# A step of the attention that takes two pieces of filling work, one unit earlier; query norms behind a weighing; four sums of a down projection behind the next weight chunks

## The chip, the cores and the metric

One core of a Trainium2 chip runs the whole program. The metric is the device time of one execution in microseconds (us); three timed runs of the kernel before gave 1322.02, 1323.74 and 1325.03. The engines are TensorE (PE, with its weight loads shown as PEld), VectorE (DVE), ScalarE (ACT), GpSimd (POOL) and SyncE (SP), which issues most transfers.

## The reference

A trunk of two layers on 512 tokens of width 1024, in float32. Layer 0 is a Mamba-2 mixer and a convolutional feed-forward block (ConvFFN); layer 1 is differential attention and a ConvFFN. Cut to what the change touches:

```python
def diff_attention(x, k, v, rel_bias, ...):
    q = rms_norm((rms_norm(x, ln_g) @ q_w).reshape(b, s, 8, 2, 64), q_norm_g)
    ...
    logits = jnp.einsum('bqhcd,bkhcd->bhcqk', qblk, k) * scale + bias     # causal mask
    p = jax.nn.softmax(logits, axis=-1)
    attn = p[:, :, 0] - lam * p[:, :, 1]          # two maps per head
    o = jnp.einsum('bhqk,bkhd->bqhd', attn, v)
    return (rms_norm(o, subln_g) * (1.0 - lam_init)).reshape(b, s, 1024) @ out_w

def conv_ffn(x, ln_g, up_w, conv_w, conv_b, down_w):
    u = causal_dwconv(rms_norm(x, ln_g) @ up_w, conv_w, conv_b)
    gate, up = u[..., :2816], u[..., 2816:]
    return (jax.nn.silu(gate) * up) @ down_w
```

## The kernel before

**Numbers.** Every matrix product is split: a weight chunk of 128x1024 is loaded (`wr_...`), ScalarE rounds it to a high half `wh_...`, VectorE subtracts to get the low half `wl_...`, and TensorE adds up three products (high by high, high by low, low by high). `chunk` (with `emit_chunk`, `Weights.split` or, for down weights, `combine`) issues the loads and splits of a chunk two chunks ahead of its use; three buffers each hold raw, high and low halves.

**Attention (layer 1).** TensorE's order here is the order of the code (`tc.manual_schedule`); the other engines' orders are made by a scheduler from the code's order and the dependencies. The 8 heads are worked off as 24 units: `Unit(h, part)`, where part 0 holds query blocks 0 and 1, part 1 block 2 and part 2 block 3. A unit passes through `logits` (products `lg`, L1498; VectorE adds the bias and takes maxima, L1504; ScalarE exponentials, L1512), `weigh` (VectorE joins the two maps, L1525, once per query block), `turn` (TensorE transposes into `at`, L1534) and `values` (products `po`, L1545, copied to `ot`, L1548). When the three units of a head are done, `normed_out` normalises the head's output `ot` (VectorE, L1558), and `turned_out` transposes it (`oT`, L1564; copies `oh` and `ol`, L1567 and L1568).

Between these small pieces TensorE does filling work: `fill` is a chain of generators for the projections `v0`, `q1`, `v1` and the first half of the output projection. Each `next(fill)` inside `proj` runs the products of one weight chunk for two of the four token blocks: twelve products (`ps_v_0` and `ps_v_1`, or `ps_v_2` and `ps_v_3`). The names `wh_v_0`, `wh_v_2` and so on count the k blocks of a chunk. A list of numbers in the loop over units (`for places in [...]`) says how many pieces each step takes. A step runs `turn` of the unit before, `logits`, `weigh`, `values` of an older unit, and then its pieces; `out_of` runs `turned_out` for a head that is due, ahead of the piece where the step has one piece, and behind its first piece where it has two.

`head_norm` belongs to `q1`, the queries of heads 4 to 7: it takes the root (`rsqrt_act`, factor `ssq`), multiplies four tiles `knq` by it on VectorE (L1350), and puts the transposes `ktq` (L1357) with their copies `qT` (L1358) into a list `late`; `proj` runs an entry of it when its place, a pair (first k block, token block), is reached. For `q1` the places are (2, 0) and (2, 1), so the transposes stand between the products of the second chunk of `v1`.

**Down projection of layer 1.** `ffn` works in three parts of feature blocks, (0, 6), (6, 14) and (14, 22). At the end of each part `down_tokens` multiplies by the down weights with seven products instead of eight (a Strassen-like scheme): `m` runs over "1257634"; the sums of products go to the residual `xr` and to a running sum `run_sum`, by VectorE (helper `add`, L1139). Products have lines L1133, L1135 and L1136. For `m == "6"` each of the two token blocks gets five sums; the last two of them, into `xr` of block 2 + b, are read by nothing near. All engines' orders here are the scheduler's.

Of the kernel before, what the change touches and what calls it, by code (L numbers as in the profile page):

```python
# [9 lines left out]
F32 = mybir.dt.float32  # L10
# [3 lines left out]
ALU = mybir.AluOpType  # L14
# [4 lines left out]
P = 128  # L19
# [3 lines left out]
NT = T // P  # L23
# [18 lines left out]
def trunk_kernel(ctx: ExitStack, tc, x, ssm_ln_g, ssm_in_w, ssm_conv_w, ssm_conv_b, ssm_dt_bias,  # L42
# [950 lines left out]
    def ffn(l, norm, bp, gnext, nnext):  # L993
        with tc.tile_pool(name="ffn_h%d" % l, bufs=1) as hp, tc.tile_pool(name="ffn%d" % l, bufs=1) as fp:
# [65 lines left out]
            def combine(key, m, p0, c, nq):  # L1060

                n = nq * ncol
                if m == "2" or (m == "4" and not l):
                    t = wrp.tile([P, 1024], F32, tag="raw", name="wr_" + key)
                    sync.dma_start(view(t, nq), source(p0, c, nq, 1, 0 if l or m == "2" else 1))
                elif l:
                    t = raws["x" if m == "7" else "y" if m == "3" else "z"][c // 2]
                    if m == "7":
                        dve.tensor_tensor(out=t[:, :n], in0=t[:, :n], in1=raws["y"][c // 2][:, :n], op=ALU.add)
                else:  # L1070
                    t = raws["x" if m in "17" else "z"][c]
                wh = wp.tile([P, 1024], F32R, tag="wh", name="wh_" + key)
                wl = wp.tile([P, 1024], F32R, tag="wl", name="wl_" + key)
                act.activation(wh[:, :n], t[:, :n], AF.Copy)
                dve.tensor_tensor(out=wl[:, :n], in0=t[:, :n], in1=wh[:, :n].bitcast(F32), op=ALU.subtract)  # L1075
                ready.append((key, view(wh, nq), view(wl, nq)))
                more = ({"1": (0, 1), "5": (1, 1), "6": (1, 0)} if l else {"1": (0, 1), "5": (0, 0), "6": (1, 0)}).get(m)
                if more:
                    plus(t, p0, c, nq, *more)
# [41 lines left out]
            def down_tokens(p0, n, sides, last):  # L1121

                nq = n // 2
                side = {"1": 0, "2": 1, "4": 2, "5": 3, "6": 4, "7": 5, "3": 6}

                def products(m, bs, qs, pss, first=True, end=True, cols=slice(0, 512)):

                    for low in range(2):
                        for b in bs:
                            for q in qs:  # L1130
                                h, w = (t[:, side[m], b * P:(b + 1) * P] for t in sides[q][:2])
                                if low:
                                    pe.matmul(pss[b], h, ws[q][1][:, cols], start=False, stop=end and q == qs[-1])  # L1133
                                    continue
                                pe.matmul(pss[b], h, ws[q][0][:, cols], start=first and q == qs[0], stop=False)  # L1135
                                pe.matmul(pss[b], w, ws[q][0][:, cols], start=False, stop=False)  # L1136

                def add(t, v, op=ALU.add):
                    dve.tensor_tensor(out=t, in0=t, in1=v, op=op)  # L1139

                def to(b, c, n=512):
                    return xr[:, b, c:c + n]

                def store(b, c, eng):
                    eng.dma_start(out[0, b * P:(b + 1) * P, c:c + 256], to(b, c, 256))

                def stores(bs, c):
                    for b in bs:
                        for j in range(2):
                            store(b, c + 256 * j, sync if j else act)  # L1150

                for m in SEVEN[1]:
                    pss = [(aux_bank if m in "273" else mm_bank)("ps_s%s_%d_%d" % (m, p0, b)) for b in range(2)]
                    cut = last and m == "4"
                    ws = {}
                    for q0 in range(0, nq, 2):
                        wh, wl = chunk("s1%s_%d_%d" % (m, p0, q0))
                        qs = range(q0, min(nq, q0 + 2))
                        for q in qs:
                            ws[q] = wh[:, q - q0, :], wl[:, q - q0, :]  # L1160
                        if not cut:
                            products(m, range(2), qs, pss, q0 == 0, qs[-1] == nq - 1)
                    if cut:
                        products(m, (0,), range(nq), pss)
                    for b in range(2):
                        r = run_sum[:, b, :]
                        if m == "1":
                            add(to(b, 0), pss[b])
                            act.activation(r, pss[b], AF.Copy)
                        elif m == "2":  # L1170
                            add(to(b, 0), pss[b])
                        elif m == "5":
                            add(to(b, 512), pss[b])
                            add(to(2 + b, 512), pss[b])
                        elif m == "7":
                            seven = pss
                        elif m == "6":
                            add(r, pss[b])
                            add(to(b, 512), r, ALU.subtract)
                            add(r, seven[b])  # L1180
                            add(to(2 + b, 512), r, ALU.subtract)
                            add(to(2 + b, 0), r)
                        elif m == "3":
                            add(to(b, 512), pss[b])
                        elif not (cut and b):
                            add(to(2 + b, 0), pss[b])
                    if last and m in "263":
                        stores((2, 3) if m == "6" else (0, 1), 0 if m == "2" else 512)
                    if cut:
                        stores((2,), 0)  # L1190
                        products(m, (1,), range(nq - 1), pss)
                        add(to(3, 0), pss[1])
                        for j in range(2):
                            end = aux_bank("end%d" % j)[:, :256]
                            products(m, (1,), [nq - 1], {1: end}, cols=slice(256 * j, 256 * (j + 1)))
                            add(to(3, 256 * j, 256), end)
                            store(3, 256 * j, act if j else sync)
# [85 lines left out]
    with tc.tile_pool(name="att", bufs=1) as ap, ExitStack() as later:  # L1283
# [61 lines left out]

        def head_norm(key, kn, ss, dst, gcol, where):
            rsqrt_act(ss, ap, key, [P, NT, 8], 64)
            for b in range(NT):
                v = kn[b].rearrange("p (a q) -> p a q", a=8)
                dve.tensor_tensor(out=v, in0=v, in1=ss[:, b, :].unsqueeze(2).to_broadcast([P, 8, 64]),  # L1350
                                  op=ALU.mult)

            def turned(bs):
                for b in bs:
# [263 lines left out]
        with tc.manual_schedule(engines={mybir.EngineType.PE}):  # L1618
# [51 lines left out]
                    values(valued)  # L1670
                    valued += 1

            for places in [(2, 2), 1, 1, 1, 1, 1, 1, 1, 1, 1, 2, 1, 1, 1, 1, 2, 1, 2, 1, 2, 1, 2, 2, 1, 1, 1]:
                if isinstance(places, tuple):
                    weigh_to(t)
                    turn_to(t - 1)
# [76 lines left out]
```

## Time and profile before

| what | value |
|---|---|
| timed runs | 1322.02, 1323.74 (median), 1325.03 us |
| the profiled execution's own time | 1323.59 us |
| its span, first to last instruction | 1321.9 us |
| mean granted TensorE clock | 0.999 |
| DMA mean | 127 GB/s |

The span is shown beside the own time because rows of the trace count from the span's start. TensorE's busy share is 99%, but a busy TensorE is not one at its peak: products are pipelined, and the trace's ends of products are modelled. So progress is read from the starts of products, and losses from the list of waits and from places where starts come further apart. In a timeline's row stand the start, the duration, the engine, line and operation, the tiles written and read, shapes and count, and in brackets the idle time ahead of it with what ended it.

### The profile page before, as it was taken

How to read it: one execution, taken by the hardware profiler on the slowest of the kernel's cores; microseconds unless marked ns; L12 is line 12 of the kernel's file. 1: busy time of each engine (PE TensorE's matmuls, PEld its weight loads, DVE VectorE, ACT ScalarE, POOL GpSimd, SP SyncE). 2: the span in 40 equal slices, each digit the busy share in tenths (PEclk: the TensorE clock that was granted, in tenths of full speed). 3: DMA queues.
4: the chain of work that ended last, by engine and by line, in shares of the span. 5: the costliest groups of instructions: out<-in, count | busy, mean ns of one | idle time of the engine just before them, and what ended most of it. 6: DMA issues, size and time to landing. Idle time of an engine off the chain costs nothing. (4 is left out here: it accounts for less than half of the span.)

```text
span 1321.9 us, 18303 instructions
## 1 busy us (share of the span) xinstructions
PE 1313.3 (99%) x6771; PEld 1097.8 (83%) x6771; DVE 1094.1 (83%) x1834; ACT 722.5 (55%) x1176; POOL 176.2 (13%) x243
## 2 busy tenths in 40 slices
PE   9999999999999999999999999999999999999998
PEld 8878888888888988898889887767888878888887
DVE  7989888788878878886889877778778978887887
ACT  6696554743454545543556676767654534444452
POOL 4330200300121401110113210000020100010001
PEclk9999999999999999999999999999999999999999
DMA  7553533532235657674856854211225445453635
GB/s 209 161 154 87 146 108 103 145 92 79 80 96 149 118 149 205 167 155 128 225 143 143 208 129 125 64 57 56 65 80 159 97 119 178 106 99 112 191 64 128
DMA packets 202553, 167.85 MB, mean 127 GB/s; under 512 B 7580, under 2 KB 175904, under 8 KB 202464
## 3 DMA queue, kind: packets, MB, share of 16 engines
q1 hardware_dynamic: 176080, 124.93, 31.8%
q0 software_dynamic: 22928, 36.46, 14.8%
q10 hardware_dynamic: 3456, 5.30, 1.1%
q8 instruction: 53, 0.87, 0.3%
q14 instruction: 36, 0.29, 0.1%
HBM read 160.21 MB, written 6.44 MB: 126 GB/s over the span
## 5 line engine op out<-in xcount | busy, mean ns | idle before, releaser
L207 PE MATMUL ps_u<-xgh,wh_u 128*128 128x512 f32 x352 | 137.4, 390 | 0.0
L209 PE MATMUL ps_g<-xgh,wl_g 128*128 128x512 f32 x352 | 137.1, 389 | 0.0
L207 PE MATMUL ps_g<-xgh,wh_g 128*128 128x512 f32 x352 | 137.1, 389 | 0.0
L209 PE MATMUL ps_u<-xgh,wl_u 128*128 128x512 f32 x352 | 137.0, 389 | 0.0
L208 PE MATMUL ps_g<-xgl,wh_g 128*128 128x512 f32 x352 | 137.0, 389 | 0.0
L208 PE MATMUL ps_u<-xgl,wh_u 128*128 128x512 f32 x352 | 136.9, 389 | 0.0
L207 PE MATMUL ps_in<-xgh,wh_in 128*128 128x512 f32 x304 | 122.9, 404 | 0.0
L209 PE MATMUL ps_in<-xgh,wl_in 128*128 128x512 f32 x304 | 119.7, 394 | 0.0
L208 PE MATMUL ps_in<-xgl,wh_in 128*128 128x512 f32 x304 | 119.1, 392 | 0.0
L209 PEld LDWEIGHTS ps_g<-xgh,wl_g 128*128 128x128 f32 x352 | 66.1, 188 | 14.0 <-DVE wl_g L158 0.3
L208 PEld LDWEIGHTS ps_g<-xgl,wh_g 128*128 128x128 f32 x352 | 66.1, 188 | 13.7
L1228 PE MATMUL ps_s<-sl,wh_s 128*128 128x256 f32 x308 | 77.5, 283 | 0.0
L209 PEld LDWEIGHTS ps_u<-xgh,wl_u 128*128 128x128 f32 x352 | 66.1, 188 | 13.7
L1227 PE MATMUL ps_s<-sh,wh_s 128*128 128x256 f32 x308 | 77.5, 283 | 0.0
L208 PEld LDWEIGHTS ps_u<-xgl,wh_u 128*128 128x128 f32 x352 | 66.1, 188 | 13.6
L207 PEld LDWEIGHTS ps_g<-xgh,wh_g 128*128 128x128 f32 x352 | 66.1, 188 | 13.6
L207 PEld LDWEIGHTS ps_u<-xgh,wh_u 128*128 128x128 f32 x352 | 66.1, 188 | 13.5
L1118 ACT ACTIVATE sh<-vg 128x256 fp32r<-128x256 f32 (+1 forms) x44 | 23.0, 524 | 96.0 <-DVE vg L1266 96.0
L1047 POOL DMA_DIRECT2D wz<-in_ffn_down_w_dram x36 | 44.2, 1295 | 233.3 <-DVE wl_s L1075 156.1
L1262 ACT ACTIVATE vg<-vg 128x512 f32<-128x512 f32 x44 | 27.8, 633 | 78.7 <-DVE vg L1019 78.7
L1019 DVE SCALAR_TENSOR_TENSOR vg<-ug,cf,vg 128x511 f32<-128x511 f32 x88 | 65.8, 748 | 5.5 <-ACT vg L1017 4.1
L147 ACT ACTIVATE wh_u<-wr_u 128x1024 fp32r<-128x1024 f32 x44 | 46.6, 1059 | 42.5 <-PE ps_g L208 35.4
(430 smaller groups left out, 3527.1 us busy)
## 6 DMA issues: line engine op xcount, KB each, us to landing
wr_g<-in_ffn_up_w_dram SPq DMA_DIRECT2D x44, 512.0 KB, 3.9
wr_u<-in_ffn_up_w_dram SPq DMA_DIRECT2D x44, 512.0 KB, 4.0
wr_in<-in_ssm_in_w_dram SPq DMA_DIRECT2D x40, 512.0 KB, 3.9
wz<-in_ffn_down_w_dram POOLq DMA_DIRECT2D x27, 512.0 KB, 5.9
m<-cumd POOLq DMA_DIRECT2D x16, 512.0 KB, 5.0
wr_out<-in_ssm_out_w_dram SPq DMA_DIRECT2D x16, 512.0 KB, 3.5
wr_s<-in_ffn_down_w_dram SPq DMA_DIRECT2D x13, 512.0 KB, 3.8
xT<-in_ffn_down_w_dram SPq DMA_DIRECT2D x10, 512.0 KB, 7.0
```

Of the source, the lines that this page charges most:

```text
L147: return act.activation(self.wh[:, :self.n], self.raw[:, :self.n], AF.Copy)
L207: pe.matmul(ps, wh, xh, start=start, stop=False)
L208: pe.matmul(ps, wh, xl, start=False, stop=False)
L209: return pe.matmul(ps, wl, xh, start=False, stop=stop).ins
L1019: dve.scalar_tensor_tensor(out=v[:, s:], in0=u[:, :T - s], scalar=col(2 - s), in1=v[:, s:], op0=ALU.mult, op1=ALU.add)
L1047: pool.dma_start(view(t, nq), source(p0, c, nq, j, i), accum_op=ALU.add)
L1118: act.activation(sh[:, o], v, AF.Copy)
L1227: pe.matmul(v[:, b], wh[:, q, cols], h, start=q == 0, stop=False)
L1228: pe.matmul(v[:, b], wh[:, q, cols], w, start=False, stop=False)
L1262: act.activation(ga, ga, AF.Silu)
```

## The change

Three things are done:

1. In the list of places the second step that takes two pieces of filling work comes one unit earlier (position 9 of the list instead of 10, counted from 0).
2. The multiplication of the query tiles `knq` of `q1` by their factor (`normed`) is no longer issued at once but put into `late` with the place (0, 3): the end of the first chunk of `v1`. In the code it so stands behind the weighing of the step that it falls into.
3. In the first part of layer 1's down projection (`p0 == 0`), the last two of the five sums for each token block at `m == "6"` move into `second_half`, called at `m == "3"` and issued behind the last low half of weights that `combine` has made by then (`state["low"]`, the chunks of `m == "4"`). The other two parts call `second_half` at the old place.

```diff
-                dve.tensor_tensor(out=wl[:, :n], in0=t[:, :n], in1=wh[:, :n].bitcast(F32), op=ALU.subtract)
+                state["low"] = dve.tensor_tensor(out=wl[:, :n], in0=t[:, :n], in1=wh[:, :n].bitcast(F32),
+                                                 op=ALU.subtract).ins
...
+                def second_half(b):
+                    r = run_sum[:, b, :]
+                    add(to(2 + b, 512), r, ALU.subtract)
+                    add(to(2 + b, 0), r)
...
                             add(r, seven[b])
-                            add(to(2 + b, 512), r, ALU.subtract)
-                            add(to(2 + b, 0), r)
+                            if p0:
+                                second_half(b)
                         elif m == "3":
+                            if not p0:
+                                with tc.issue_after(state["low"]):
+                                    second_half(b)
                             add(to(b, 512), pss[b])
...
         def head_norm(key, kn, ss, dst, gcol, where):
             rsqrt_act(ss, ap, key, [P, NT, 8], 64)
-            for b in range(NT):
-                v = kn[b].rearrange("p (a q) -> p a q", a=8)
-                dve.tensor_tensor(out=v, in0=v, in1=ss[:, b, :].unsqueeze(2).to_broadcast([P, 8, 64]),
-                                  op=ALU.mult)
+            def normed():
+                for b in range(NT):
+                    v = kn[b].rearrange("p (a q) -> p a q", a=8)
+                    dve.tensor_tensor(out=v, in0=v, in1=ss[:, b, :].unsqueeze(2).to_broadcast([P, 8, 64]),
+                                      op=ALU.mult)
+
+            if key == "q1":
+                late.append(((0, 3), normed))
+            else:
+                normed()
...
-            for places in [(2, 2), 1, 1, 1, 1, 1, 1, 1, 1, 1, 2, 1, 1, 1, 1, 2, 1, 2, 1, 2, 1, 2, 2, 1, 1, 1]:
+            for places in [(2, 2), 1, 1, 1, 1, 1, 1, 1, 1, 2, 1, 1, 1, 1, 1, 2, 1, 2, 1, 2, 1, 2, 2, 1, 1, 1]:
```

No instruction is added or taken away. How the instructions stand, before and after, at the places where the order differs (the changed kernel's lines are some 9 to 15 higher there; numbers of buffers differ too):

TensorE in the attention, before, from the last products `po` of a unit on; of the twelve products of a piece of filling work the first and the last are shown:

```order
L1545 MATMUL po_1_8281<-vt_6963,at_1_8180 128x128
L1564 MATMUL oT_8286<-ident,ot_8028 128x128 x4
L1325 MATMUL ps_v_2_8234<-wh_v_0_7964,xgh 128x512
...
L1327 MATMUL ps_v_3_8235<-wh_v_0_7964,xgl 128x512
L1534 MATMUL at_0_8308<-ident,lg_0_0_8192 128x128 x3
L1498 MATMUL lg_2_0_8317<-kT_6957,qT_6959 128x512
...
L1327 MATMUL ps_v_0_8232<-wh_v_2_8088,xgl 128x512
L1357 MATMUL ktq_0_8350<-ident,knq_0_8106 128x128 x4
```

The same place in the changed kernel:

```order
L1560 MATMUL po_1_8277<-vt_6963,at_1_8180 128x128
L1334 MATMUL ps_v_2_8230<-wh_v_0_7964,xgh 128x512
...
L1336 MATMUL ps_v_3_8231<-wh_v_0_7964,xgl 128x512
L1579 MATMUL oT_8298<-ident,ot_8028 128x128 x4
L1334 MATMUL ps_v_0_8228<-wh_v_2_8088,xgh 128x512
...
L1372 MATMUL ktq_0_8321<-ident,knq_0_8106 128x128 x4
L1372 MATMUL ktq_1_8327<-ident,knq_1_8111 128x128 x4
...
L1549 MATMUL at_0_8352<-ident,lg_0_0_8192 128x128 x3
L1513 MATMUL lg_2_0_8361<-kT_6957,qT_6959 128x512
```

`oT` has moved behind twelve products, and the first half of the next chunk, with all sixteen `ktq` transposes, ahead of `at_0` and the next logits.

VectorE at the same place, before, from the normalisation of the head's output on:

```order
L1558 TENSOR_TENSOR ot_8028<-ot_8028,so_8168 128x512
L498 SCALAR_TENSOR_TENSOR rst_q_8221<-rst_q_8221,rsm_q_8220 128x32
L1521 SCALAR_TENSOR_TENSOR sm_0_8191<-sm_0_8191,nlam,rc_0_8276 128x2
L499 SCALAR_TENSOR_TENSOR ssq_7751<-rst_q_8221,ssq_7751 128x32
L1525 SCALAR_TENSOR_TENSOR lg_0_0_8192<-lg_0_1_8193,sm_0_8191,lg_0_0_8192 128x128
L1350 TENSOR_TENSOR knq_0_8106<-knq_0_8106,ssq_7751 128x512
L1350 TENSOR_TENSOR knq_1_8111<-knq_1_8111,ssq_7751 128x512
L1350 TENSOR_TENSOR knq_2_8157<-knq_2_8157,ssq_7751 128x512
L1350 TENSOR_TENSOR knq_3_8162<-knq_3_8162,ssq_7751 128x512
L1525 SCALAR_TENSOR_TENSOR lg_0_0_8192<-lg_0_1_8193,sm_0_8191,lg_0_0_8192 128x256
L1568 SCALAR_TENSOR_TENSOR ol_8292<-oT_8286,c_89,oh_8291 128x512
```

In the changed kernel:

```order
L1573 TENSOR_TENSOR ot_8028<-ot_8028,so_8168 128x512
L498 SCALAR_TENSOR_TENSOR rst_q_8221<-rst_q_8221,rsm_q_8220 128x32
L1536 SCALAR_TENSOR_TENSOR sm_0_8191<-sm_0_8191,nlam,rc_0_8272 128x2
L499 SCALAR_TENSOR_TENSOR ssq_7751<-rst_q_8221,ssq_7751 128x32
L1540 SCALAR_TENSOR_TENSOR lg_0_0_8192<-lg_0_1_8193,sm_0_8191,lg_0_0_8192 128x128
L1540 SCALAR_TENSOR_TENSOR lg_0_0_8192<-lg_0_1_8193,sm_0_8191,lg_0_0_8192 128x256
L1360 TENSOR_TENSOR knq_0_8106<-knq_0_8106,ssq_7751 128x512
L1360 TENSOR_TENSOR knq_1_8111<-knq_1_8111,ssq_7751 128x512
L1360 TENSOR_TENSOR knq_2_8157<-knq_2_8157,ssq_7751 128x512
L1360 TENSOR_TENSOR knq_3_8162<-knq_3_8162,ssq_7751 128x512
L1583 SCALAR_TENSOR_TENSOR ol_8304<-oT_8298,c_89,oh_8303 128x512
```

The weighing of the 128x256 block stands ahead of the four norms instead of behind them.

VectorE in the first down part of layer 1, before, from the sums into the running sum for `m == "6"` on (`wl_s_0_0_10097` and `wl_s_0_2_10113` are the low halves for `m == "4"`):

```order
L1139 TENSOR_TENSOR run_sum_9342<-run_sum_9342,ps_s_0_0_10026 128x512
L1139 TENSOR_TENSOR run_sum_9342<-run_sum_9342,ps_s_0_1_10027 128x512
L1139 TENSOR_TENSOR xr<-xr,run_sum_9342 128x512 x4
L1075 TENSOR_TENSOR wl_s_0_0_10097<-wz_0_9340,wh_s_0_0_10096 128x1024
L1075 TENSOR_TENSOR wl_s_0_2_10113<-wz_1_9341,wh_s_0_2_10112 128x512
L1139 TENSOR_TENSOR xr<-xr,ps_s_0_0_10094 128x512
L1139 TENSOR_TENSOR xr<-xr,ps_s_0_1_10095 128x512
L158 TENSOR_TENSOR wl_g_6_10129<-wr_g_6_10126,wh_g_6_10128 128x1024
```

In the changed kernel:

```order
L1140 TENSOR_TENSOR run_sum_9342<-run_sum_9342,ps_s_0_0_10026 128x512
L1140 TENSOR_TENSOR run_sum_9342<-run_sum_9342,ps_s_0_1_10027 128x512
L1075 TENSOR_TENSOR wl_s_0_0_10093<-wz_0_9340,wh_s_0_0_10092 128x1024
L1075 TENSOR_TENSOR wl_s_0_2_10109<-wz_1_9341,wh_s_0_2_10108 128x512
L1140 TENSOR_TENSOR xr<-xr,run_sum_9342 128x512 x2
L1140 TENSOR_TENSOR xr<-xr,ps_s_0_0_10090 128x512
L1140 TENSOR_TENSOR xr<-xr,run_sum_9342 128x512 x2
L1140 TENSOR_TENSOR xr<-xr,ps_s_0_1_10091 128x512
L158 TENSOR_TENSOR wl_g_6_10129<-wr_g_6_10126,wh_g_6_10128 128x1024
```

The four sums have moved behind the two low halves and between the adds of `m == "3"`, still ahead of `wl_g_6`, the low half of the next gate chunk. TensorE's order changes there by one move: two products of `ps_g_6` (L207 and L208), which stood ahead of the products with `wl_s_0_0_10097`, now stand behind all products of `m == "4"`, just ahead of two of `ps_u_6` and of `ps_g_6`'s first product with `wl_g_6` (L209).

## The prediction

> **What bounds the kernel now.** I read the page's totals first, then TensorE's list of waits, then TensorE's timeline around the two entries of that list that lie in places the change touches. All times are from one profiled execution: its span is 1321.9 us and its own time 1323.59 us, so 1.69 us lie around the span; the three timed runs have a median of 1323.74 us. I make the sum against 1323.59 and the comparison against 1323.74.
>
> ```profile
> span 1321.9 us, 18303 instructions
> PE 1313.3 (99%) x6771; PEld 1097.8 (83%) x6771; DVE 1094.1 (83%) x1834; ACT 722.5 (55%) x1176; POOL 176.2 (13%) x243
> PE oT L1564 <- DVE ot L1558: 2.8, 1, 2.8
> PE warm L291 <- DVE ones L218: 1.1, 1, 1.1
> PE ps_s L1133 <- DVE wl_s L1075: 0.7, 1, 0.7
> ```
>
> The first two rows are of the page, the last three are the whole list of TensorE's waits (total, times, longest). TensorE is the bound, and it waits only three times. One is at the start. The other two are the transposes `oT` of a head's output, which wait for VectorE's normalisation `ot`, and the products of the first down part of layer 1, which wait for a low half `wl_s`. The change moves something at exactly these two places, so the time can change by what TensorE loses there and by little else.
>
> **The attention place: what is lost now.** TensorE's timeline (start, duration, line, tiles, count, and in brackets the idle time before it with what ended it), with an undisturbed step beside it:
>
> ```profile
> 847.30 0.60 PE L1564 MATMUL oT<-ident,ot 128*128 128x128 f32 x4
> 847.66 0.47 PE L1325 MATMUL ps_q<-wh_q,xgh 128*128 128x512 f32 x1
> ...
> 857.01 0.94 PE L1545 MATMUL po<-vt,at 128*128 128x128 f32 x6
> 857.70 0.47 PE L1325 MATMUL ps_v<-wh_v,xgh 128*128 128x512 f32 x1
> ...
> 860.54 0.60 PE L1534 MATMUL at<-ident,lg 128*128 128x128 f32 x4
> ...
> 861.91 0.94 PE L1545 MATMUL po<-vt,at 128*128 128x128 f32 x6
> 865.61 1.03 PE L1564 MATMUL oT<-ident,ot 128*128 128x128 f32 x4 [2.76 <-DVE ot L1558]
> 866.30 0.78 PE L1325 MATMUL ps_v<-wh_v,xgh 128*128 128x512 f32 x1
> ...
> 870.46 0.49 PE L1534 MATMUL at<-ident,lg 128*128 128x128 f32 x3
> ...
> 880.23 0.49 PE L1534 MATMUL at<-ident,lg 128*128 128x128 f32 x3
> ```
>
> Undisturbed, the work after six `po` products starts 0.69 us after them (857.01 to 857.70), twelve `ps_v` products take 2.84 (857.70 to 860.54) and `oT` takes 0.36 (847.30 to 847.66). So at the stalled place TensorE could have gone on at 861.91 + 0.69 = 862.60, and `oT` with twelve products would have taken 3.20. They end at 870.46, 7.86 after 862.60: 4.66 us are lost. Of these 865.61 - 862.60 = 3.01 are the wait. The other 1.65 come after it, and the rows of stretches (busy time by engine, then granted clock) say why:
>
> ```profile
> 855.00:860.00 5.00, 5.00 (x31) 3.91 (x31) 3.62 (x13) 4.81 (x11) 0.00 (x0) 1.00 0.20 54
> 866.00:869.00 3.00, 3.00 (x10) 2.43 (x9) 3.00 (x7) 0.99 (x3) 0.00 (x0) 0.50 0.01 3
> ```
>
> The granted clock is 1.00 in the undisturbed step and 0.50 for three microseconds behind the wait. The list of waits shows 2.8 us; the loss is two thirds larger.
>
> **The attention place: what is lost after.** The change puts the second half of a value chunk (the twelve products of `ps_v_2` and `ps_v_3`) between `po` and `oT`. They run from 862.60 to 865.44: their banks and their weights were ready in the old order too, as they ran straight behind `oT`. VectorE's order up to `ot` is unchanged:
>
> ```profile
> 864.87 0.68 DVE L1558 TENSOR_TENSOR ot<-ot,so 128x512 f32<-128x512 f32 x1
> ...
> 865.83 0.35 DVE L1525 SCALAR_TENSOR_TENSOR lg<-lg,sm,lg 128x128 f32<-128x128 f32 x1
> 866.10 2.49 DVE L1350 TENSOR_TENSOR knq<-knq,ssq 128x512 f32<-128x512 f32 x4
> 868.50 0.48 DVE L1525 SCALAR_TENSOR_TENSOR lg<-lg,sm,lg 128x256 f32<-128x256 f32 x1
> 868.90 0.74 DVE L1568 SCALAR_TENSOR_TENSOR ol<-oT,c,oh 128x512 fp32r<-128x512 f32 x1
> ```
>
> `ot` ends at 865.55 and `oT` can start at 865.61 as before; the wait shrinks from 3.01 to 865.61 - 865.44 = 0.17, too short for the clock to fall. Then comes what is new on the path: the first half of the next chunk, with the transposes `ktq` of the query norms in it, now stands one step earlier. Its durations, from where it ran before:
>
> ```profile
> 872.86 0.48 PE L1325 MATMUL ps_v<-wh_v,xgh 128*128 128x512 f32 x1
> ...
> 874.33 1.04 PE L1357 MATMUL ktq<-ident,knq 128*128 128x128 f32 x8
> 875.12 0.47 PE L1325 MATMUL ps_v<-wh_v,xgh 128*128 128x512 f32 x1
> ```
>
> Six products take 1.47 and eight `ktq` transposes 0.79. So `oT` ends at 865.97, `ktq_0` can start at 867.44, `ktq_1` at 867.84, `ktq_2` at 869.7. VectorE must have the norms by then. It now weighs the 128x256 block first (0.40, from 868.50 to 868.90), so the four norms start at 866.10 + 0.40 = 866.50, 0.60 apart (2.40 for four), each 0.69 long: they end at 867.19, 867.79, 868.39 and 868.99. The margins are 0.25, 0.05 and 1.3: covered, though barely for the second; I allow 0.1 for it. If VectorE were later by d, TensorE would wait about d here. The weighing itself moves earlier by 2.4, and its reader, the transposes `at`, comes at 870.5 as before, by then with 12 products and 16 transposes more behind it. That is the gain: 4.66 - 0.17 - 0.1 = 4.4 us.
>
> Does the lead last? TensorE then reaches the next steps 4.4 earlier, and VectorE must follow. Its idle times in the stretch that is squeezed:
>
> ```profile
> 871.42 0.75 DVE L173 SCALAR_TENSOR_TENSOR wl_v<-wr_v,c,wh_v 128x512 fp32r<-128x512 f32 x1 [1.70 <-ACT wh_v L172]
> 877.20 0.16 DVE L497 TENSOR_TENSOR rst_o<-so 128x4 f32<-128x4 f32 x1 [0.27 <-ACT so L496]
> 881.52 1.22 DVE L158 TENSOR_TENSOR wl_ao<-wr_ao,wh_ao 128x1024 fp32r<-128x1024 f32 x1 [3.04 <-ACT wh_ao L147]
> ...
> 870.66 0.72 ACT L172 ACTIVATE wh_v<-wr_v,c 128x512 fp32r<-128x512 f32 x1 [3.29 <-PE ps_v L1327]
> 875.60 1.24 ACT L1358 ACTIVATE qT<-ktq,c 128x512 f32<-128x512 f32 x2
> ```
>
> The three of VectorE add to 5.01, and the two large ones end with copies of ScalarE that wait for TensorE's buffers, which now come free earlier. 5.0 is more than 4.4, by 0.6: enough, but this is the tightest cover of the forecast. ScalarE gets the four copies `qT` (0.62 each, 1.24 for two) ahead of the copy of `at`; they fit into the 3.29 us that it idles there, which costs nothing as long as `ktq` is on time. The queues of SP and POOL keep their order, and no transfer is moved past another.
>
> **The first down part of layer 1.** Rows of TensorE, VectorE and ScalarE:
>
> ```profile
> 1064.14 0.39 PE L207 MATMUL ps_g<-xgh,wh_g 128*128 128x512 f32 x1
> 1065.48 1.21 PE L1133 MATMUL ps_s<-wl_s,sh 128*128 128x512 f32 x4 [0.72 <-DVE wl_s L1075]
> 1068.42 0.50 PE L209 MATMUL ps_g<-xgh,wl_g 128*128 128x512 f32 x1
> ...
> 1061.80 2.49 DVE L1139 TENSOR_TENSOR xr<-xr,run_sum 128x512 f32<-128x512 f32 x4
> 1064.21 1.82 DVE L1075 TENSOR_TENSOR wl_s<-wz,wh_s 128x1024 fp32r<-128x1024 f32 x2
> 1065.95 1.28 DVE L1139 TENSOR_TENSOR xr<-xr,ps_s 128x512 f32<-128x512 f32 x2
> 1067.14 1.22 DVE L158 TENSOR_TENSOR wl_g<-wr_g,wh_g 128x1024 fp32r<-128x1024 f32 x1
> ...
> 1060.97 1.07 ACT L1074 ACTIVATE wh_s<-wz 128x1024 fp32r<-128x1024 f32 x1 [4.13 <-DMA wz<-in_ffn_down_w_dram]
> ```
>
> Now four sums (2.41, from 1061.80 to 1064.21) stand ahead of the two low halves, and TensorE waits. After the change the low halves come first. They need `wh_s`, which ends at 1062.04, and take 1.74 (1064.21 to 1065.95): ready at 1063.2 and 1063.8, ahead of TensorE at 1064.14. That wait goes. But the sums don't go: they now stand ahead of `wl_g`, which TensorE needs next. VectorE: 1062.04 + 1.74, four sums 2.41, two adds of products 1.19 (1065.95 to 1067.14), gives 1067.38 as the start of `wl_g`, 0.24 later than now. TensorE starts `ps_g` L209 0.06 behind its end: 1068.66 against 1068.42. TensorE itself would be there at 1064.14 + 14 products of 0.23 = 1067.36. So a wait of 0.72 is replaced by one of 1.3, 0.24 us later on the path. I take +0.24. The bounds: -1.06 if `wl_g` were no wait at all, and +1.9 if the wait of 1.3 halved the clock as the one above did (0.24 + 1.65).
>
> **The sum.** 1323.59 - 4.4 + 0.24 = 1319.4 us.
>
> [...] The clock fell to 0.50 behind a wait of 2.8 us (row 866 to 869) and not behind one of 0.72. [...]
>
> **The rivals.**
>
> (1) *The clock falls once more*, price 1.65 (above): 1321.1. Place one is the wait of 1.3 before `ps_g`, between a wait that did halve the clock (2.76) and one that did not (0.72), nearer to the latter. Place two is the new row of transposes: 4 `oT`, 16 `ktq` and 3 `at` between only 12 products. Against that speaks the stretch where 16 `ktq` ran with 18 products at clock 1.00:
>
> ```profile
> 872.00:877.00 5.00, 5.00 (x34) 4.39 (x33) 4.86 (x15) 4.17 (x11) 0.00 (x0) 1.00 0.17 50
> ```
>
> [...]
>
> (2) *VectorE or ScalarE becomes the bound* behind the attention place, since the cover is 5.0 against 4.4: half of the lead, 2.2, is returned as waits of `at`, `lg` or `po`: 1321.6.
>
> (3) *The whole lead is returned* in the same way, so that the change doesn't bring what it moves: 1323.59 + 0.24 = 1323.8.
>
> (4) *Slower*: the transposes `ktq` take the place of `oT` as the waiting ones. The norms now stand behind the weighing, and `ktq` comes 6.9 earlier. If VectorE is held there by w, TensorE waits w, and from about 2.8 the clock falls too: from there 1319.4 + w + 1.65 is above the old time (1323.9 at w = 2.8), and w = 6 gives 1327.1. It would need a norm to end near 870 instead of 867.2; every input of it (maxima, exponentials, the factor `ssq`) is there by 865.8 in the rows above, so I give it little.
>
> (5) *More than forecast*: `wl_g` makes nobody wait in the down part: 1319.4 - 1.3 = 1318.1.
>
> **How the numbers follow.** Forecast 0.61, (5) 0.09, (1) 0.10, (2) 0.09, (3) 0.07, (4) 0.04. The range reaches from (5) less 0.3 for the scatter of a median, 1317.8, to (2) with 0.2 of it, 1321.8, and leaves out (3) and (4). A measurement of this kernel can tell about 0.2%, 2.65 us, from no change: faster is below 1321.1, slower above 1326.4. Faster: the forecast and (5), half of (1), and 0.04 of (2), together 0.79. Slower: (4). The rest, 0.17, is within.
>
> **What would show it.** In TensorE's list of waits `oT` is gone or under 0.4, a new entry `ps_g` <- `wl_g` of 1.1 to 1.3 stands in place of `ps_s` <- `wl_s`, and `ktq` waits under 0.2. The granted clock stays 1.00 in the five microseconds behind `oT`. From the start of the `po` that now starts at 861.91 to the `at` that now starts at 880.23 TensorE takes 13.9 us instead of 18.3. It would be wrong if the clock row behind `ps_g` or `ktq` shows 0.50, if `at`, `lg` or `po` appear as waiting for VectorE or ScalarE with over 1 us, or if `ktq` waits longer than `oT` did.

## The result and the profile after

| | before | changed |
|---|---|---|
| median of nine timed executions | 1323.74 us (1322.02 to 1325.03) | 1319.74 us (1319.20 to 1320.68) |
| the profiled execution, its span | 1323.59, 1321.9 us | 1319.76, 1318.1 us |

The ratio of the two is 0.9971, with a 95% interval from 0.9963 to 0.9980: the medians differ by 4.0 us, and the interval reaches from 2.6 to 4.9. The forecast was 1319.4, in a range from 1317.8 to 1321.8.

The page's totals of the changed kernel:

```profile
span 1318.1 us, 18304 instructions
PE 1311.3 (99%) x6771; PEld 1095.9 (83%) x6771; DVE 1094.6 (83%) x1834; ACT 722.5 (55%) x1176; POOL 178.5 (14%) x243
```

The five engines have as many instructions as before; the total is one higher (18304 against 18303), and what the one is the page doesn't say. TensorE's whole list of waits (total, times, longest):

```profile
PE ps_g L209 <- DVE wl_g L158: 1.3, 1, 1.3
PE warm L291 <- DVE ones L218: 1.1, 1, 1.1
PE ps_s L1136 <- ACT wh_s L1074: 0.2, 1, 0.2
```

The entry of `oT`, 2.8 us, is gone. In place of `ps_s` <- `wl_s` (0.7) stands `ps_g` <- `wl_g` (1.3), and there is a small new one behind the high half `wh_s`. The attention place in TensorE's timeline:

```profile
861.64 0.94 PE L1560 MATMUL po<-vt,at 128*128 128x128 f32 x6
...
865.34 0.65 PE L1579 MATMUL oT<-ident,ot 128*128 128x128 f32 x4
...
867.22 1.04 PE L1372 MATMUL ktq<-ident,knq 128*128 128x128 f32 x8
...
869.48 1.03 PE L1372 MATMUL ktq<-ident,knq 128*128 128x128 f32 x8
...
870.35 0.49 PE L1549 MATMUL at<-ident,lg 128*128 128x128 f32 x3
...
875.67 0.49 PE L1549 MATMUL at<-ident,lg 128*128 128x128 f32 x3
```

`oT` starts 3.70 us after `po` (861.64 to 865.34), exactly as before (861.91 to 865.61), but TensorE now works through that time: there is no idle time in brackets. From `po` to the last `at` shown, which are the ends of the forecast's own test, it takes 14.03 us; before it was 18.32, from 861.91 to 880.23. The granted clock (third number from the right in a row of a stretch) behind `oT`, and in the down part behind its new wait:

```profile
866.00:869.00 3.00, 3.00 (x18) 2.54 (x18) 3.00 (x6) 2.98 (x6) 0.00 (x0) 1.00 0.00 0
869.00:872.00 3.00, 3.00 (x19) 1.92 (x17) 2.67 (x7) 1.77 (x4) 0.00 (x0) 1.00 0.02 3
1064.00:1068.00 4.00, 3.34 (x15) 2.78 (x16) 4.00 (x5) 0.00 (x0) 0.00 (x0) 1.00 0.52 144
```

It is 1.00 in all three. The down part, TensorE first, then ScalarE and VectorE:

```profile
1057.28 0.61 PE L1134 MATMUL ps_s<-wl_s,sh 128*128 128x512 f32 x2
1058.06 0.50 PE L1136 MATMUL ps_s<-wh_s,sh 128*128 128x512 f32 x1 [0.17 <-ACT wh_s L1074]
...
1062.96 0.39 PE L208 MATMUL ps_u<-xgl,wh_u 128*128 128x512 f32 x1
1064.66 0.50 PE L209 MATMUL ps_g<-xgh,wl_g 128*128 128x512 f32 x1 [1.31 <-DVE wl_g L158]
...
1056.95 1.06 ACT L1074 ACTIVATE wh_s<-wz 128x1024 fp32r<-128x1024 f32 x1 [4.69 <-DMA wz<-in_ffn_down_w_dram]
...
1049.01 1.83 DVE L1075 TENSOR_TENSOR wl_s<-wz,wh_s 128x1024 fp32r<-128x1024 f32 x2
...
1058.04 1.83 DVE L1075 TENSOR_TENSOR wl_s<-wz,wh_s 128x1024 fp32r<-128x1024 f32 x2 [0.74 <-ACT wh_s L1074]
1059.79 1.29 DVE L1140 TENSOR_TENSOR xr<-xr,run_sum 128x512 f32<-128x512 f32 x2
...
1063.39 1.22 DVE L158 TENSOR_TENSOR wl_g<-wr_g,wh_g 128x1024 fp32r<-128x1024 f32 x1
...
1074.95 0.69 DVE L1016 TENSOR_TENSOR uu<-ps_u,nr_f 128x512 f32<-128x512 f32 x1 [1.45 <-PE ps_u L209]
```

Read backwards from L209: it waits for `wl_g`, which stands behind the adds and the sums, these behind `wl_s`, that behind `wh_s`, and `wh_s` starts when the transfer into `wz` lands. VectorE idles for 0.74 us in front of `wl_s`, where before it was working off the four sums. So everything from 1056.95 to 1064.66 now follows the landing of one transfer. GpSimd issues it behind the first of the two low halves of `m == "6"`, which are the last readers of its buffers. Counted from the end of both (1049.01 + 1.83 = 1050.84), as in every profile below, the transfer took 6.11 us until `wh_s` starts.

For the experiments I use one length in all profiles: from the last pair of `ps_s` products with `wl_s` in the down block of `m == "3"` (the expectations call it the third) to the add `uu`, which comes when the next gate and up chunks are through. TensorE's work between the two, 68 products, is the same in every kernel. In the changed kernel it is 1074.95 - 1057.28 = 17.67 us. Before:

```profile
1061.85 0.62 PE L1133 MATMUL ps_s<-wl_s,sh 128*128 128x512 f32 x2
...
1053.73 1.83 DVE L1075 TENSOR_TENSOR wl_s<-wz,wh_s 128x1024 fp32r<-128x1024 f32 x2
...
1078.76 0.69 DVE L1016 TENSOR_TENSOR uu<-ps_u,nr_f 128x512 f32<-128x512 f32 x1 [1.45 <-PE ps_u L209]
```

16.91 us; the transfer took 5.41, from 1055.56 to the start of `wh_s` at 1060.97. The down part therefore cost 0.76 in this profile where the forecast had 0.24, and the attention place brought 4.29 where it had 4.4.

### The profile page after: what moved, and what is told of

It reads as the page before. It is cut to its first block, busy times and chain, and to the rows that moved or that the text cites. A ratio compares the mean times of both kernels' runs of the same rounds, so it can differ in the third digit from the quotient of the medians.

```text
span 1318.1 us, 18304 instructions
## 1 busy us (share of the span) xinstructions
PE 1311.3 (99%) x6771; PEld 1095.9 (83%) x6771; DVE 1094.6 (83%) x1834; ACT 722.5 (55%) x1176; POOL 178.5 (14%) x243
## 4 chain that ended last, share of the span: by engine, by line
PE 97%; DMA 1%; DVE 1%; issue 0%; ACT 0%; DVEq 0%; SPq 0%; POOLq 0%; ACTq 0%
PE ps_g L209 6%; PE ps_u L209 6%; PE ps_g L208 6%; PE ps_u L208 6%; PE ps_g L207 6%; PE ps_u L207 6%; PE ps_in L207 5%; PE ps_in L209 5%; PE ps_in L208 5%; PE ps_s L1234 3%; PE ps_s L1237 3%; PE ps_s L1236 3%; PE ps_o L208 2%; PE ps_o L207 2%; PE ps_o L209 2%; PE ps_s L1136 2%
## 5 line engine op out<-in xcount | busy, mean ns | idle before, releaser
L209 PE MATMUL ps_g<-xgh,wl_g 128*128 128x512 f32 x352 | 137.1, 389 | 1.3 <-DVE wl_g L158 1.3
L207 PE MATMUL ps_u<-xgh,wh_u 128*128 128x512 f32 x352 | 137.4, 390 | 0.0
L207 PE MATMUL ps_g<-xgh,wh_g 128*128 128x512 f32 x352 | 137.0, 389 | 0.0
L208 PE MATMUL ps_g<-xgl,wh_g 128*128 128x512 f32 x352 | 137.0, 389 | 0.0
L209 PE MATMUL ps_u<-xgh,wl_u 128*128 128x512 f32 x352 | 137.0, 389 | 0.0
L208 PE MATMUL ps_u<-xgl,wh_u 128*128 128x512 f32 x352 | 136.9, 389 | 0.0
L207 PE MATMUL ps_in<-xgh,wh_in 128*128 128x512 f32 x304 | 122.9, 404 | 0.0
L209 PE MATMUL ps_in<-xgh,wl_in 128*128 128x512 f32 x304 | 119.7, 394 | 0.0
L208 PE MATMUL ps_in<-xgl,wh_in 128*128 128x512 f32 x304 | 119.2, 392 | 0.0
L209 PEld LDWEIGHTS ps_g<-xgh,wl_g 128*128 128x128 f32 x352 | 66.1, 188 | 15.4 <-DVE wl_g L158 1.7
L209 PEld LDWEIGHTS ps_u<-xgh,wl_u 128*128 128x128 f32 x352 | 66.1, 188 | 13.7
L208 PEld LDWEIGHTS ps_g<-xgl,wh_g 128*128 128x128 f32 x352 | 66.1, 188 | 13.7
L207 PEld LDWEIGHTS ps_g<-xgh,wh_g 128*128 128x128 f32 x352 | 66.1, 188 | 13.6
L208 PEld LDWEIGHTS ps_u<-xgl,wh_u 128*128 128x128 f32 x352 | 66.1, 188 | 13.6
L207 PEld LDWEIGHTS ps_u<-xgh,wh_u 128*128 128x128 f32 x352 | 66.1, 188 | 13.5
```

The source lines that it names most:

```text
L207: pe.matmul(ps, wh, xh, start=start, stop=False)
L208: pe.matmul(ps, wh, xl, start=False, stop=False)
L209: return pe.matmul(ps, wl, xh, start=False, stop=stop).ins
```

## The experiments

**The attention parts alone.** The down part is put back:

```diff
-                            if p0:
-                                second_half(b)
+                            second_half(b)
                         elif m == "3":
-                            if not p0:
-                                with tc.issue_after(state["low"]):
-                                    second_half(b)
                             add(to(b, 512), pss[b])
```

> The changed kernel with the four sums of the first down part back in front of the two low halves: the attention parts of the change alone. Theory (the whole gain is the stall at oT, 4.3 us in the trace, and the down part gives 0.2 to 0.8 of it back): 1323.74 - 4.3 = 1319.4, at most the time of the full change, 1319.74, and in TensorE's list of waits ps_s <- wl_s of 0.7 stands again in place of ps_g <- wl_g. Rival (the down part gains what its old wait showed, 0.72, and the attention place less): 1320.4 or more.

Measured: 1319.6 us against 1323.39 of the kernel before on the same chip, ratio 0.9972 (0.9962 to 0.9982). Its waits of TensorE:

```profile
PE warm L291 <- DVE ones L218: 1.1, 1, 1.1
PE ps_s L1134 <- DVE wl_s L1075: 0.8, 1, 0.8
```

The old wait of the down part is back, and the gain is the whole gain. The rival (1320.4 or more) falls. Its median is 0.1 us below that of the full change, which times can't tell apart.

**The down part alone**, on the kernel before.

> The kernel before with the down part of the change alone; the attention place keeps its order and its wait. Theory: the wait of 0.72 at ps_s <- wl_s is replaced by one of about 1.3 at ps_g <- wl_g, and the time is 1323.74 + 0.24 = 1324.0 by the forecast's term, 1324.5 if the 0.8 that the changed kernel's trace shows is the true size. Rival (the old wait was the whole price): 1323.74 - 0.72 = 1323.0. Second point: the wait of wh_s for the transfer into wz. If it is 5.4 us from the end of wl_s to the start of wh_s as before, the 0.24 holds; if it is 6.1 as in the changed kernel, the longer transfer belongs to this part of the change.

Measured: 1324.2 us against 1323.39, ratio 1.0005 (0.9996 to 1.0014). The theory lies within the interval; the rival, 0.72 less, would be 0.9995, just outside it. The timelines are plainer:

```profile
1062.68 0.61 PE L1134 MATMUL ps_s<-wl_s,sh 128*128 128x512 f32 x2
...
1069.80 0.50 PE L209 MATMUL ps_g<-xgh,wl_g 128*128 128x512 f32 x1 [1.30 <-DVE wl_g L158]
...
1062.08 1.06 ACT L1074 ACTIVATE wh_s<-wz 128x1024 fp32r<-128x1024 f32 x1 [4.41 <-DMA wz<-in_ffn_down_w_dram]
...
1080.14 0.69 DVE L1016 TENSOR_TENSOR uu<-ps_u,nr_f 128x512 f32<-128x512 f32 x1 [1.45 <-PE ps_u L209]
```

The length is 17.46, 0.55 more than before: this part loses time, it doesn't gain the 0.72. From `wh_s` to L209 it takes 7.72 (7.71 in the changed kernel; the forecast's chain gave 7.69, from 1060.97 to 1068.66). The transfer took 5.60 us, neither the 5.41 of before nor the 6.11 of the changed kernel.

**The list of places alone** and **the norms alone**, each on the kernel before:

```diff
-            for places in [(2, 2), 1, 1, 1, 1, 1, 1, 1, 1, 1, 2, 1, 1, 1, 1, 2, 1, 2, 1, 2, 1, 2, 2, 1, 1, 1]:
+            for places in [(2, 2), 1, 1, 1, 1, 1, 1, 1, 1, 2, 1, 1, 1, 1, 1, 2, 1, 2, 1, 2, 1, 2, 2, 1, 1, 1]:
```

> The kernel before with the list of places alone: the first two-step place a unit earlier, the query norms in their old place ahead of the second weighing, the down part as before. Theory: the same as the attention parts alone, within 0.2 us (1319.4), since the second weighing then ends with the norms at about 868.9 and its reader, the transposes at, comes at 870.5; the move of the norms is worth nothing by itself. Rival (the norms had to go behind the weighing so that at or ol is on time): a wait of at or of the next head's work of 1 us or more, 1320.5 or more.

> The kernel before with the query norms behind the second weighing, and nothing else of the change. Theory: VectorE's order up to ot is the same, so the wait of oT stays at 2.8 with half the clock behind it, and the time is that of the kernel before within 0.3 us. Rival (the norms delayed oT or ktq): the wait of oT changes by 0.4 or more, or ktq waits.

Measured: the places 1319.51 us, ratio 0.9971 (0.9959 to 0.9982); the norms 1324.2 against 1323.85, ratio 1.0001 (0.9992 to 1.0010). The timeline of TensorE with the places alone:

```profile
862.25 0.94 PE L1545 MATMUL po<-vt,at 128*128 128x128 f32 x6
865.94 0.66 PE L1564 MATMUL oT<-ident,ot 128*128 128x128 f32 x4
...
876.28 0.49 PE L1534 MATMUL at<-ident,lg 128*128 128x128 f32 x3
```

14.03 us, the same as in the full change, so one moved number carries all of it; `at` doesn't wait, which was the rival. With the norms alone the wait of `oT` stays at 2.8, and `ktq` doesn't wait: the second part of the change does nothing that can be measured, by itself or beside the places.

**The sums behind the next gate and up weights.** The changed kernel, with `state["low"]` also set by the low halves of the gate and up chunks, and:

```diff
                         elif m == "3":
-                            if not p0:
-                                with tc.issue_after(state["low"]):
-                                    second_half(b)
                             add(to(b, 512), pss[b])
                         elif not (cut and b):
+                            if not p0:
+                                with tc.issue_after(state["low"]):
+                                    second_half(b)
                             add(to(2 + b, 0), pss[b])
```

> The changed kernel with the four sums of the first down part moved further, behind the low halves of the next gate and up weights (wl_g and wl_u), so that only the two adds of products stand ahead of wl_g on VectorE. Theory: wl_g then ends at about 1062.3 and TensorE comes to it at 1062.7, so the wait of 1.31 goes and nothing takes its place: 1319.74 - 1.3 = 1318.4, below both kernels. Rival (VectorE is late with the next halves instead, or the order that the scheduler gives TensorE moves the wait): a new wait of 0.7 us or more within the next 15 us and a time of 1319.2 or more.

Measured: 1317.89 us against 1323.39, ratio 0.9960 (0.9947 to 0.9972). TensorE's list of waits holds only the one at the start. The place, TensorE and VectorE:

```profile
1057.32 0.61 PE L1136 MATMUL ps_s<-wl_s,sh 128*128 128x512 f32 x2
...
1062.31 0.39 PE L211 MATMUL ps_g<-xgh,wl_g 128*128 128x512 f32 x1
...
1060.56 1.22 DVE L158 TENSOR_TENSOR wl_g<-wr_g,wh_g 128x1024 fp32r<-128x1024 f32 x1
...
1072.94 0.69 DVE L1018 TENSOR_TENSOR uu<-ps_u,nr_f 128x512 f32<-128x512 f32 x1 [1.55 <-PE ps_u L211]
```

(L211 is what L209 is in the other kernels.) `wl_g` ends at 1061.78, half a microsecond ahead of TensorE, and the length is 15.62: 1.29 less than before and 2.05 less than in the changed kernel's profile. More went than the 1.31 of the list, for these two waits cost more than their idle time. In the changed kernel L209 starts 1.70 us behind the product ahead of it, where 0.23 is usual: 1.47 lost. The wait for `wh_s`, 0.17 in its row, puts the next product 0.78 behind the start of the last `wl_s` pair, where 0.45 is usual: 0.33 lost. The first product behind each of the two waits is followed after 0.34 instead of 0.23, which is 0.22 together. The three add to 2.02 of the 2.05.

**The changed kernel again, and the last one again, on one chip.**

> The changed kernel once more, unaltered, beside the next one on the same chip, for one more sample of the transfer into wz that the down part now hangs on. In ten profiles so far the step from the end of TensorE's third down block to the sum uu took 16.9 us in the seven with the old order of the sums and 17.67 and 17.46 in the two with the new one; those two had wh_s 0.33 and 0.60 us ahead of the end of that block (0.88 in the kernel before). Theory (the chain from wh_s to L209 is fixed at 7.7 us, and the landing of the transfer sets where it begins): 7.7 again, and a step that is longer or shorter than 17.6 by just as much as wh_s starts later or earlier than in those. Rival (the new order delays the transfer itself): wh_s 6.1 us or more behind the last wl_s. Time 1319.2 to 1320.2.

> The kernel with the four sums behind wl_g and wl_u once more, on the same chip as the changed kernel. Theory: the step from the third down block to uu takes 15.6 us whatever the landing of the transfer (up to 0.5 later than in its first profile), and the time is lower than that of the changed kernel by 17.6 - 15.6 = 2.0, at 1317.5 to 1318.3. Rival (the first result was a lucky draw): within 0.7 of the changed kernel.

Measured: the changed kernel 1319.72 us, ratio 0.9974 (0.9965 to 0.9982); the sums behind the weights 1318.29 us, ratio 0.9963 (0.9951 to 0.9976). The second is lower by 1.4, not by the 2.0 expected. A reason that fits stands in the profile of the changed kernel:

```profile
1058.54 0.61 PE L1134 MATMUL ps_s<-wl_s,sh 128*128 128x512 f32 x2
...
1065.45 0.49 PE L209 MATMUL ps_g<-xgh,wl_g 128*128 128x512 f32 x1 [1.29 <-DVE wl_g L158]
...
1057.73 1.06 ACT L1074 ACTIVATE wh_s<-wz 128x1024 fp32r<-128x1024 f32 x1 [4.21 <-DMA wz<-in_ffn_down_w_dram]
...
1075.73 0.69 DVE L1016 TENSOR_TENSOR uu<-ps_u,nr_f 128x512 f32<-128x512 f32 x1 [1.45 <-PE ps_u L209]
```

Here the length is 17.19, and `wh_s` starts 0.81 ahead of TensorE's row; its transfer took 5.53. The other kernel has 15.62 again, which leaves 1.57 between the two. Only one execution of each shows its length, so that the medians follow it is likely and not shown. All fourteen profiles of this study, by the order of the sums:

| order | profiles | start of `wh_s` ahead of the last `wl_s` pair of `m == "3"` | length to `uu` |
|---|---|---|---|
| old | 9 | 0.66 to 1.14 | 16.86 to 16.91 |
| of the change | 3 | 0.33, 0.60, 0.81 | 17.67, 17.46, 17.19 |
| behind `wl_g`, `wl_u` | 2 | 0.79, 0.91 | 15.62, 15.62 |

In the old order the length doesn't depend on the start of `wh_s`, over the half microsecond that these profiles cover; in that of the change it follows it one to one (0.33 + 17.67, 0.60 + 17.46 and 0.81 + 17.19 are 18.00, 18.06 and 18.00). The rival, that the new order delays the transfer itself, falls: it took 5.60 and 5.53 in the two other profiles with the new order, and the 6.11 was not seen again. That the third order doesn't depend on the transfer is not shown, since both its profiles had an early one. By its rows, an estimate: a landing as late as in the changed kernel's first profile would be 0.46 later (0.79 - 0.33), `wl_g` would still be ready, with 0.53 to spare, and only the 0.33 that TensorE lost in front of `wh_s` would come back. All ten times of the third order lie at or below 1319.19, the twenty of the changed kernel at or above 1319.17.

**What the stall cost besides its length.** This is the kernel before, with products added ahead of `oT` that do no useful work; `spare` is the bank of `ps_v_2`, which the following products overwrite, `w` their high weights, set where a projection takes a new chunk, and N is 12, 6 or 3; with the transposes, 28 of a key tile stand in their place:

```diff
+            if h == 1:
+                spare, w = state["fill"]
+                for i in range(N):
+                    pe.matmul(spare, xgh[i % 2][:, 0:P], w[:, i % 2, :], start=True, stop=True)
             ps = aux_bank("oT%d" % h)
```

> The kernel before with twelve added products in the wait of oT (the kind and the weights of the ps_v products that follow, written into the bank that those overwrite). They do no useful work and last 2.84 us, so oT starts where it did, but TensorE isn't idle. Theory (1.65 of the 4.66 lost is a clock of 0.50 that follows the idle time): oT starts at the same distance from po, the granted clock stays 1.00 behind it, the way from po to the at that comes two steps later falls from 18.32 to 16.67 us and the time by 1.65. Rival (the 1.65 is work that waits for something else, VectorE or a bank): the way stays 18.3 and the time doesn't change.

> As with the twelve added products, but with six: the idle time ahead of oT is 1.6 us, between the 1.31 that kept the clock at 1.00 in the changed kernel and the 2.76 that halved it. If the length of the idle time decides with a bound above 1.6: the clock stays 1.00 and the time is that of the twelve products (-1.65). If the bound lies below 1.6, or a part of the loss goes with the idle time: clock 0.50 for a while, and a time between that of the kernel before and -1.65.

> As with the twelve added products, but with 28 transposes of 128x128 (of a key tile, into the same bank) in the wait of oT, about 2.8 us by the 0.79 that eight ktq take. If transposes hold the clock as products do: clock 1.00 behind oT and -1.65, as with the products. [...]

> As with the six added products in the wait of oT, but with three, so that the idle time ahead of oT is about 2.1 us, between the 1.36 that kept the clock at 1.00 and the 2.76 that halved it. If a bound above 2.1 decides: clock 1.00 and 16.85 us from po to the at two steps later. If it lies below: clock 0.50 for about 3 us and 18.3. No theory of mine favours one.

> The kernel with three added products in the wait of oT once more. Its ten times fell into two groups, six from 1321.62 to 1322.29 and four from 1323.66 to 1324.24, 1.4 us and more apart; the profiled execution, with the clock at 0.50 behind an idle time of 2.1 us, was of the upper one. Theory (an idle time of 2.1 us halves the clock in some executions and not in others, by when it falls, so no single length is the bound): two groups again, about 1.7 us apart in their middles, and a profiled execution of the lower group shows an idle time of 2.1 with the clock at 1.00 behind it and 16.85 us from po to the at two steps later. Rival (a fixed bound below 2.1 us; the groups come from elsewhere): a profiled execution of the lower group too has the clock at 0.50 there and 18.3 us.

| added | idle ahead of `oT` | `po` to `at` | clock behind `oT` | median (range) | ratio (interval) |
|---|---|---|---|---|---|
| 12 products | none | 16.84 | 1.00 | 1322.36 (1321.86 to 1323.06) | 0.9990 (0.9982 to 0.9999) |
| 28 transposes | none | 17.04 | 1.00 | 1322.66 (1321.91 to 1323.62) | 0.9992 (0.9983 to 1.0000) |
| 6 products | 1.36 | 16.85 | 1.00 | 1322.51 (1321.91 to 1324.39) | 0.9990 (0.9981 to 0.9999) |
| 3 products | 2.08 | 18.32 | 0.50 | 1322.22 (1321.62 to 1324.24) | 0.9995 (0.9986 to 1.0004) |
| 3, again | 2.06 | 16.80 | 1.00 | 1322.29 (1321.61 to 1324.57) | 0.9995 (0.9986 to 1.0004) |

Adding twelve or six products makes the kernel faster, if only by 0.1% with intervals that end at 0.9999; for the transposes and for three products the interval doesn't exclude that nothing changed. The rows with twelve products, TensorE and then the stretch behind `oT`:

```profile
862.42 0.94 PE L1546 MATMUL po<-vt,at 128*128 128x128 f32 x6
...
866.11 0.66 PE L1569 MATMUL oT<-ident,ot 128*128 128x128 f32 x4
...
879.26 0.49 PE L1535 MATMUL at<-ident,lg 128*128 128x128 f32 x3
```

```profile
866.00:869.00 3.00, 2.99 (x16) 2.47 (x16) 3.00 (x9) 1.50 (x5) 0.00 (x0) 1.00 0.01 3
```

`oT` starts where it did (3.69 us behind `po`), and the way to `at` is 1.48 shorter than 18.32. The last two rows of the table are one and the same kernel. Its first profiled execution, the wait in TensorE's timeline and then the stretch behind it:

```profile
865.77 0.98 PE L1569 MATMUL oT<-ident,ot 128*128 128x128 f32 x4 [2.08 <-DVE ot L1559]
```

```profile
866.00:869.00 3.00, 3.00 (x10) 2.52 (x9) 3.00 (x7) 1.15 (x3) 0.00 (x0) 0.50 0.01 3
```

And the second, in the same two views:

```profile
865.27 0.66 PE L1569 MATMUL oT<-ident,ot 128*128 128x128 f32 x4 [2.06 <-DVE ot L1559]
```

```profile
866.00:869.00 3.00, 3.00 (x15) 2.22 (x13) 3.00 (x6) 0.92 (x2) 0.00 (x0) 1.00 0.01 3
```

Nearly the same idle time is followed once by half the clock and once by the full one. The times fall into two groups: 1321.61 to 1322.77 (seven) and 1323.61 to 1324.57 (four) in the second run of it, six and four in the first; the profile with half the clock is of an upper group, the other of a lower. The mean granted clocks agree: half the clock for three microseconds of 1322 takes 0.001 off the mean of an execution (an estimate), and the upper groups have 0.998 or 0.999, the lower ones 0.999 or 1.000. A high time alone is no sign of it, though: the profiled execution with six products took 1324.39 us, with the clock at 1.00 behind `oT`.

One profile each of N = 12, 6 and 3 would have been read as a bound somewhere between 1.36 and 2.08. The second profile of N = 3 leaves for a fixed bound only the gap from 2.06 to 2.08, which these two profiles can't exclude. A sign against it comes from the kernel before. Its wait was 2.76 in all three profiles of this place with nothing added and the old list (before, the down part alone, the norms alone), each time with the clock reduced behind it (0.50 in the row of the kernel before; in the other two, products behind it start 0.43 us apart instead of 0.23). Yet of its 88 executions timed beside the experiments eleven have a mean clock of 1.000 and a median of 1322.1 us, the other 77 at most 0.999 and 1323.9. If the eleven had the same wait, which no profile shows, a wait of 2.76 too doesn't always halve the clock.

## Why the prediction was right, and where it was off

*The attention place, -4.4.* Right in mechanism and size: -4.29. `ot` stayed where it was, TensorE's work went in front of it, and `oT` lost its idle time. The split of the old loss into 3.01 of wait and 1.65 of clock holds too, with the second at 1.48 in the trace of the twelve added products, and 1.3 by the times (0.9990 of 1323.85, within 0.1 and 2.4). What the forecast didn't know is that the 1.65 isn't paid in every execution: with three added products it was paid in one profile and not in the other, and the mean clocks make this likely for the kernel before. That a row of transposes lowers the clock, the second place of rival (1), no run shows. The forecast's row of 16 `ktq` at clock 1.00 said little on it, since 18 products stand among them; the run with 28 transposes in the wait, at 1.00 behind `oT`, says more, and the changed kernel's rows from 866 to 872 are at 1.00 too.

*ktq, -0.1 allowed.* No entry of `ktq` stands in the changed kernel's list of waits. The part that the norms were moved for needed no help: the places alone bring the same.

*The lead lasts.* Behind the place neither `at`, `lg` nor `po` waits for VectorE or ScalarE, so rivals (2) and (3) didn't come, and the cover of 5.0 us against 4.4 was enough. Rival (4) would have shown as a wait of `ktq`; there is none.

*The down part, +0.24.* This is the term that was mis-sized in the changed kernel's profile: 0.76. The chain was right to 0.02 us (7.71 from `wh_s` to L209, forecast 7.69). The step that failed is the one that took 1062.04 as the end of `wh_s` and so tied its start to TensorE, as the one profile of before showed it. In the old order VectorE had the four sums to work off when the transfer landed, and starts of `wh_s` spread over half a microsecond (0.66 to 1.14 ahead of TensorE) moved nothing. In the new order nothing lies between the landing and `wl_g` but the chain, so the landing decides: 0.28 lost in the changed kernel's second profile (17.19 against 16.91), 0.55 with this part alone, 0.76 in the first profile. At the landing of before (0.88 ahead) the length would be 18.0 - 0.88 = 17.1, and the term would have stood. The forecast's two bounds for it weren't reached: the new wait of 1.3 didn't halve the clock in any of the three profiles (1.00 in the changed kernel's row; in the other two the products behind it start 0.23 to 0.24 apart; rival (1)), and it didn't vanish (rival (5)) until the sums were moved further.

*The sum.* By the first profile -4.29 + 0.76 is -3.5, and the stretches before the attention place were 0.27 shorter in that execution (`po` at 861.64 instead of 861.91), together the 3.8 between the spans. That the 0.27 hid half of the 0.52 by which the down part was mis-sized is luck. The forecast's 1319.4 and the median of 1319.74 differ by less than the 1.5 us over which single executions scatter.

## What to carry to other kernels

When work is moved away from in front of a late instruction, look at what that work was covering: here the four sums covered the scatter of a transfer (5.41 to 5.63 us in the six profiles of the old order where it sets the start of `wh_s`), and moved behind the low halves they only passed their wait on to the next weights, while one chunk further they cost nothing and the kernel ran at 1317.9 to 1318.3. A wait of TensorE, where it bounds the kernel, can cost more than its length (here another 1.5 us in clock behind 2.08 and 2.76 us), so fill it with work that is there anyway; of a change in three parts, run each alone before calling any of them needed. Where a gain hangs on a transfer or on the clock, take more than one profile before reading a bound or a size from it.

## What the runs showed of the hardware beyond this

- The granted clock fell to 0.50 for about three microseconds behind an idle time of 2.08 us in one execution and stayed at 1.00 behind one of 2.06 us in another of the same kernel. Behind 0.72 us (the kernel before, stretch 1064 to 1069 below), 1.31 (the changed kernel) and 1.36 (six products) it was 1.00, behind 2.76 (the kernel before) 0.50. What made the difference between the two executions is open.

```profile
1064.00:1069.00 5.00, 4.28 (x19) 2.96 (x17) 5.00 (x7) 2.12 (x2) 0.00 (x0) 1.00 0.00 0
```

- Twenty-eight transposes in the wait, of 128x128 in float32 against the identity, kept the clock at 1.00 in the one profile, as products did (17.04 us on the way, 0.20 more than with the products; `oT` itself starts 0.14 later behind them), and all eleven executions have a mean clock of 0.999 or 1.000.
- From the end of the last low half of `m == "6"` to the start of `wh_s`, which the transfer into `wz` sets in eleven of the fourteen profiles, it took from 5.29 to 5.70 us in thirteen, and 6.11 in one. In the 40 us ahead of it SyncE and GpSimd issue their transfers in the same order in the profile of the kernel before (5.41) and in the changed kernel's first (6.11), and the changed kernel's second profile had 5.53; what delayed that one is open.
